# Two layers of a hybrid attention trunk: the second score product of each head over all 128 rows

## The chip, the cores and the metric

The kernel runs on one core of one Trainium2 chip. The metric is device time in microseconds (us) of one execution; the kernel before takes 760.22 us, the median of three runs (759.8, 760.22 and 763.26).

## The reference

The program computes two decoder layers over 512 tokens of width 1024, in float32, and a last norm. With h the residual, each layer is:

```
u = rmsnorm(h) @ w_in             # splits into qa ka va ga qd kd vd gd, 512 columns each
oa = 8 heads of 64: causal softmax(qa ka^T / 8) with a dilated-window mask, times va
od = 4 heads: (softmax(q1 k1^T / 8) - lam * softmax(q2 k2^T / 8)) times vd, then a norm
h = h + concat(oa * silu(ga), od * silu(gd)) @ w_out
h = h + (p @ w_ple) * sigmoid(rmsnorm(h) @ w_gate)
```

The first 16 channels of each 64 of q and k get a rotary embedding. Seen as scores, a layer has 16 heads of 64 channels: 8 in the differential mixer (two for each of its 4 heads) and 8 in the dilated one.

## The kernel before, in words

All products carry float32 operands in two parts: a high part in a rounded 32-bit format and a low part, which is the remainder. A product of two such operands takes three passes, high by high, high by low, low by high (`PASSES`).

The tensor engine's work is cut into units. A unit of projection (`unit`, L237 to L251) is 24 matmuls with 512 columns each (L248). A layer has 48 units in 12 chunks of 512 output columns, in the order of `SEQ`: v, q and k of the differential mixer (units 0 to 11), v, q and k of the dilated mixer (12 to 23), the two gates, the output product, the embedding's gate. The weights of a chunk come in four pairs of row blocks: SyncE (SP) loads a pair, ScalarE (ACT) writes the high part into a ring of five slots (L200), GpSimd (POOL), and VectorE (DVE) in one case out of eight after the start, subtracts to get the low part (L203).

Attention is laid between the projection's matmuls. Each of the 16 heads of a layer has a place near its own unit: `QD` for the differential heads (7.6 to 14.6), `QA` for the dilated ones (19.6 to 26.6). A head's score work (`softmax_rows`) is four blocks of 128 queries; block i has 128 * (i + 1) keys. Blocks 0 and 1 stand together, blocks 2 and 3 stand alone, each after a few projection matmuls. The scores of a block are two matmuls into the same bank (L392, L393). DVE then masks them and takes the extreme of each row (L399), ACT takes exp and the row sums (L404), DVE scales (L445, or L478 and L479, where two heads are combined). About 1.5 units after a head's scores, the tensor engine transposes the probabilities (L427), ACT and DVE split them into two parts (L431, L434), and the products with v follow (L456 for dilated heads, L495 for differential ones).

Two heads share a pair of 64-row halves. When the projection of q or k for a pair is finished (`qk_done`), DVE shuffles and multiplies (L552, L553), POOL adds the rotary part (L556, L557), ACT writes the high part to a staging tile (L560), DVE the low part (L563), and SP copies parts to where the scores read them (`move`, L178). For a pair, `QK` holds five tiles of 128 rows by 512 tokens. Tiles 0 and 1 are q of the two heads: high part in the head's own 64 rows, low part in the other 64. Tiles 2 and 3 hold the high part of k twice, so that one matmul over 128 rows gives both high by high and low by high (L392). Tile 4 holds the low part of k of both heads, written there by DVE directly, head e in rows 64e to 64e + 63. The high part of q by the low part of k is the second matmul (L393), over the head's own 64 rows. `QK` has two such buffers, for alternate pairs.

The order of instructions on each engine is fixed by hand: every piece has a place and a length in us, and `Plan.run` sorts them by those. Nothing is reordered afterwards. SP's queue carries all transfers, weights and the copies of q and k alike.

At the start, `setup` clears two tiles on DVE and builds the identity for transposes on POOL, while the first loads are on their way; eleven matmuls warm the tensor engine's clock up.

Of the kernel before, what the change touches and what calls it, by code (L numbers as in the profile page):

```python
# [9 lines left out]
F32 = mybir.dt.float32  # L10
F32R = mybir.dt.float32r
# [19 lines left out]


def const_tables():
    """Tables that depend on the shapes alone: rotary angles by channel and position, and the
    additive masks of the scores."""
    half = ROPE_DIM // 2
    inv = np.power(np.float32(ROPE_THETA),
                   -np.arange(half, dtype=np.float32) * np.float32(2.0 / ROPE_DIM)).astype(np.float32)
    ang = (np.arange(S, dtype=np.float32)[:, None] * inv[None, :]).astype(np.float32)
    cos, sin = np.cos(ang).T, np.sin(ang).T  # L40
    c = np.ones((128, S), np.float32)
    s = np.zeros((128, S), np.float32)
    for h in (0, 64):
        c[h:h + half] = cos
        c[h + half:h + ROPE_DIM] = cos
        s[h:h + half] = -sin
        s[h + half:h + ROPE_DIM] = sin
    r = np.arange(128)[:, None]
    k = np.arange(512)[None, :]
    dist = 384 + r - k  # L50
    mult = (((dist >= 0) & (dist <= 128)).astype(np.int64) + ((dist >= 0) & (dist % 4 == 0))
            + ((dist >= 0) & (dist % 16 == 0)))
    ma = np.where(mult > 0, 8.0 * np.log(np.maximum(mult, 1)), NEG).astype(np.float32)
    md = np.where(dist >= 0, 0.0, NEG).astype(np.float32)
    return np.ascontiguousarray(np.stack([c, s, ma, md], axis=1))


class Plan:
    """The order of the instructions. The tensor engine's pieces of work have a place t, counted in
    units of projection, and a length in us; the other engines' work has a place and a distance in us  # L60
    from the time at which the tensor engine gets there when nothing holds it."""

    def __init__(self):
        self.pieces, self.items = [], []
# [18 lines left out]
            f(*a)  # L83


# A layer's chunks of 512 columns, in their order; each is four units of projection.
SEQ = ["vd", "d0", "d1", "va", "a0", "a1", "gd", "ga", "o0", "o1", "p0", "p1"]
# Where the heads' scores, their transposed probabilities and the products with v come.
QD = [7.6, 8.6, 9.6, 10.6, 11.6, 12.6, 13.6, 14.6]
QA = [19.6, 20.6, 21.6, 22.6, 23.6, 24.6, 25.6, 26.6]  # L90
LT, LP, LO = 1.5, 2.15, 1.3
# Passes of a product of two operands in two parts.
PASSES = ((0, 0), (0, 1), (1, 0))
# Columns where the blocks of keys of a transposed head begin.
TO = [0, 512, 896, 1152]


def trunk(tc, x, p, attn_gain, w_in, w_out, lq1, lk1, lq2, lk2, subln, ple_gain, w_gate, w_ple,
          final_gain, tables, out):
    nc = tc.nc  # L100
# [4 lines left out]
    with tc.tile_pool(name="sb", bufs=1) as sb, tc.tile_pool(name="ps", bufs=1, space=PSUM) as psp, \  # L105
# [3 lines left out]
        RING = sb.tile([128, NPAIR, 2, 2, 512], F32R, name="ring")  # L109
        NSTG = 3  # L110
        STG = sb.tile([128, NSTG, 2, 512], F32, name="stg")
        QK = sb.tile([128, 2, 5, 512], F32R, name="qk")
        NT = sb.tile([128, 3, 512], F32R, name="nt")
        FR = sb.tile([128, 12 * 512], F32, name="fr")
        PT = sb.tile([128, 2, 1280], F32R, name="pt")
# [61 lines left out]
        def move(dst, src):  # L177
            nc.sync.dma_start(dst.bitcast(F32), src.bitcast(F32))  # L178

# [1 line left out]
        loads = []  # L181

        def add_pair(t, us, src, hi, lo, eng):
            loads.append((t, us, src, hi, lo, eng))

        def stage(n):
            # the fourth pair comes while the others are still on their way
            return OF[:, 4:6, :] if n == NSTG else STG[:, (n - (n > NSTG)) % NSTG]

        def emit_loads():  # L190
# [40 lines left out]
                return RING[:, slots[kb // 2], lo, kb % 2, :]  # L231
            return w

# [1 line left out]
        nunit = [0]  # L235

        def unit(s, w, ureg, kind, idx, done, k0=0, cols=slice(0, 512), length=1.0):  # L237
# [12 lines left out]
                pe(s + length * i / 8, 0.648 * length, part, i)  # L250
            done(s + 0.99 * length, o)  # L251

# [1 line left out]
        def sumsq(t, h, eng=ACT):  # L254
            acc = SS[:, 2 * t + h:2 * t + h + 1]
            if eng is ACT:
# [36 lines left out]
        def load_gain(i, src):  # L293
            nc.sync.dma_start(GN[i], src.partition_broadcast(128))

# [1 line left out]
        def setup():  # L297
            DVE.memset(PT[:, 0, 0:512].bitcast(F32), 0.0)
            DVE.memset(NHALF, -0.5)
            ACT.activation(ST[:, 132:136], NHALF, AF.Exp)  # L300
            make_identity(nc, IDT)

# [7 lines left out]
        def first_gain():  # L310
            POOL.partition_broadcast(GN[0], GROW)

        # the tensor engine's clock rises while the first loads are on their way
        def warm_up():
            b = bank()
            for i in range(NWARM):
# [24 lines left out]
                                         tmp[:, 2 * l:2 * l + 1], op0=OP.add, op1=OP.subtract)  # L341
                DVE.tensor_scalar(GSUB[l], GSUB[l], 0.5 * (1.0 - li), None, op0=OP.mult)

        # times from the start of the tensor engine's first work
        def st(us, f, *a):
            at(-10, 60 + us, f, *a)

# [18 lines left out]
                at(t - 1, 0.1 * h, sumsq, t, h, (ACT, DVE)[h])  # L366
            norm_T(t - 1, 1.0, t - 0.2, t, GN[0], 0)

# [1 line left out]
        nP = [0]  # L370
        nst = [0]

        def softmax_rows(b, pr, e, mask):
            """Scores of one head for all queries, masked, with their maximum; exp and its sums."""
            r = {}
            buf = QK[:, pr % 2]
            q, k1, k2 = buf[:, e], buf[:, 2 + e], buf[:, 4]
            a = slice(64 * e, 64 * e + 64)

            def qk(i):  # L380
                if i == 0:
                    r["P"] = PB[nP[0] % 3]
                    nP[0] += 1
                    s = HST[:, 16 * (nst[0] % 4):16 * (nst[0] % 4) + 16]
                    nst[0] += 1
                    r["m"], r["d"], r["r"] = (s[:, 4 * j:4 * j + 4] for j in range(3))
                if i in (0, 2, 3):
                    r["b"] = bank()
                o = r["b"][:, 128:384] if i == 1 else r["b"][:, 0:(i + 1) * 128]
                r[i] = o  # L390
                n = (i + 1) * 128
                mm(o, q[:, i * 128:(i + 1) * 128], k1[:, 0:n], start=True, stop=False)  # L392
                mm(o, q[a, i * 128:(i + 1) * 128], k2[a, 0:n], start=False, stop=True)  # L393

            def pq(i):
                return r["P"][:, QOFF[i]:QOFF[i] + (i + 1) * 128]

            def mx(i):
                DVE.tensor_tensor_reduce(pq(i), r[i], mask[:, 512 - (i + 1) * 128:], scale=-0.125,  # L399
                                         scalar=3.0e38, op0=OP.add, op1=OP.min,  # L400
                                         accum_out=r["m"][:, i:i + 1])

            def ex(i):
                ACT.activation(pq(i), pq(i), AF.Exp, bias=r["m"][:, i:i + 1], scale=-1.0,  # L404
                               accum_out=r["d"][:, i:i + 1])

            def rec():
                DVE.reciprocal(r["r"], r["d"])
            for i in range(4):
                pe(b + (0.0, 0.01, 0.13, 0.26)[i], (0.11, 0.22, 0.33, 0.43)[i], qk, i)  # L410
                at(b + (0.01, 0.01, 0.13, 0.26)[i], 0.1 + 0.05 * i, mx, i)
                at(b + 0.26, (0.3, 0.7, 1.2, 1.8)[i], ex, i)
            at(b + 0.26, 2.6, rec)
            r["pq"] = pq
            return r

        def transposed(tb, r):
            """P transposed, by block of keys, in two parts."""
            bk = {}
            W, O = [512, 384, 384], [0, 512, 896]  # L420

            def tr(g):
                bk[g] = bank()
                c = 0
                for j in ((0,), (1,), (2, 3))[g]:
                    for i in range(j, 4):
                        nc.tensor.transpose(bk[g][:, c:c + 128], r["pq"](i)[:, j * 128:(j + 1) * 128], IDT)  # L427
                        c += 128

            def hi(g):  # L430
                ACT.activation(PT[:, 0, O[g]:O[g] + W[g]], bk[g][:, :W[g]], AF.Copy)  # L431

            def lo(g):
                DVE.tensor_sub(PT[:, 1, O[g]:O[g] + W[g]], bk[g][:, :W[g]], PT[:, 0, O[g]:O[g] + W[g]])  # L434
            for g in range(3):
                pe(tb + 0.13 * g, (0.436, 0.327, 0.327)[g], tr, g)
                at(tb + 0.13 * g, 0.1, hi, g)
                at(tb + 0.13 * g, 0.65, lo, g)
# [98 lines left out]
            pe(e + LO, 0.436, tr)  # L537
            at(e + LO, 0.1, ev3)

# [1 line left out]
        SHUF = list(range(8, 16)) + list(range(8)) + list(range(16, 32))  # L541
        nrt = [0]

        def qk_done(pr, isk):
            def done(t, o):
                r = {}
# [13 lines left out]
                    ACT.activation(NT[:, 2 * isk], r[0][0], AF.Copy)  # L560

                def lo():
                    DVE.tensor_sub(buf[:, 4] if isk else NT[:, 1], r[0][0], NT[:, 2 * isk])  # L563

                # each head's stack of 128 rows: both parts of q, and the high part of k twice
                def place_hi():
                    for e in range(2):
                        src = NT[64 * e:64 * e + 64, 2 * isk]
# [73 lines left out]
                    at(s, 1.9, sumsq, t, h)  # L642
            return done

        # the last tile of tokens: its last columns in two steps, the norm's gain before its scale
        def last_norm(s):
            a, b = slice(0, 256), slice(256, 512)
            acc = [SS[:, 8 + i:9 + i] for i in range(2)]
# [30 lines left out]
            at(s + 0.99, 1.9, scale)  # L679
            at(s + 0.99, 2.0, finish)  # L680

# [1 line left out]
        for l in range(DEPTH):  # L683
            B = UNITS * l
            X, Y = l % 2, 1 - l % 2
# [84 lines left out]
                for e in range(2):  # L770
                    head_a(l, B, pr, e, Y)

            # h of the residual comes back
            def reload(t, l=l):
                nc.sync.dma_start(HT(t), (x2 if l == 0 else hsave)[t * 128:(t + 1) * 128, :])
            for t in range(T):
                at(B + 29.6 + 0.1 * t, 0, reload, t)

            # the layer's own embedding in two parts, halved for the gate's form, and its weights
            def load_p(l=l):  # L780
                nc.sync.dma_start(PTF, p[l])

# [21 lines left out]


def layout(name, a):
    """Weights as the chunks of 512 columns that the program loads, each partition's part of two
    blocks of rows in one run; p with its channels first."""
    a = np.asarray(a)
    if name == "p":  # L810
        a = a[:, 0].transpose(0, 2, 1).reshape(DEPTH, 2, 128, S).transpose(0, 2, 1, 3)
# [30 lines left out]
```

## Time and profile before

| what | value |
|---|---|
| median of the runs | 760.22 us |
| profiled execution: span from the first to the last instruction | 758.0 us |
| around that span, by the median of the runs | 2.2 us |
| tensor engine matmul busy | 732.0 us, 97% of the span |
| DVE, ACT, POOL busy | 59%, 45%, 46% |
| granted tensor clock, mean | 0.986 |
| L392 and L393, number of matmuls | 128 and 128 |

The profile gives no other time of the profiled execution than its span, so the 2.2 us around it are the median less the span. Busy times of the tensor engine (PE) overlap, because one matmul starts before the one ahead of it has left the array: what a matmul costs is read from the distance between its start and the next start. PEld is the loading of the stationary operand, which can run under the matmul ahead.

### The profile page before, as it was taken

How to read it: one execution, taken by the hardware profiler on the slowest of the kernel's cores; microseconds unless marked ns; L12 is line 12 of the kernel's file. 1: busy time of each engine (PE TensorE's matmuls, PEld its weight loads, DVE VectorE, ACT ScalarE, POOL GpSimd, SP SyncE). 2: the span in 40 equal slices, each digit the busy share in tenths (PEclk: the TensorE clock that was granted, in tenths of full speed). 3: DMA queues.
4: the chain of work that ended last, by engine and by line, in shares of the span. 5: the costliest groups of instructions: out<-in, count | busy, mean ns of one | idle time of the engine just before them, and what ended most of it. 6: DMA issues, size and time to landing. Idle time of an engine off the chain costs nothing.

```text
span 758.0 us, 9739 instructions
## 1 busy us (share of the span) xinstructions
PE 732.0 (97%) x3379; PEld 574.2 (76%) x3379; DVE 445.4 (59%) x935; ACT 342.1 (45%) x739; POOL 352.3 (46%) x275
## 2 busy tenths in 40 slices
PE   2899999999999999999999999999999999999996
PEld 1677777787777787888888767778777778788885
DVE  0874877557785653462473387756677665346344
ACT  2343364735565632453343246563456473335321
POOL 1357464268460514572364755516837042467132
PEclk7799999999999999999999999999999999999998
DMA  5425524036350154440341453403534114543102
GB/s 222 145 83 134 148 76 126 29 111 181 71 147 20 57 195 166 140 138 29 138 155 69 140 153 83 125 29 112 166 71 147 35 57 172 189 139 116 51 29 83
DMA packets 30882, 84.78 MB, mean 112 GB/s; under 512 B 5617, under 2 KB 5617, under 8 KB 30834
## 3 DMA queue, kind: packets, MB, share of 16 engines
q1 hardware_dynamic: 30834, 84.17, 35.9%
q8 instruction: 26, 0.43, 0.2%
q14 instruction: 22, 0.18, 0.1%
HBM read 63.18 MB, written 4.19 MB: 89 GB/s over the span
## 4 chain that ended last, share of the span: by engine, by line
PE 88%; issue 4%; DVE 3%; POOL 2%; ACT 1%; DMA 1%; SPq 0%; POOLq 0%; DVEq 0%
PE b L248 66%; PE b L393 6%; PE b L392 3%; PE b L427 3%; PE b L456 3%; PE b L495 3%; PE b L726 3%; POOL ring L203 2%; PE b L280 2%; DVE fr L268 1%; DMA stg<-in_w_in_dram 1%; ACT ring L200 1%; POOL st L265 0%; DVE of L607 0%; DVE ring L203 0%
## 5 line engine op out<-in xcount | busy, mean ns | idle before, releaser
L203 POOL TENSOR_TENSOR ring<-stg,ring 128x512 fp32r<-128x512 f32 x164 | 234.8, 1461 | 200.7 <-ACT ring L200 188.1
L248 PE MATMUL b<-xy,ring 128*128 128x512 f32 x1152 | 307.2, 404 | 0.6 <-POOL ring L203 0.6
L248 PE MATMUL b<-ring,xy 128*128 128x512 f32 (+1 forms) x1176 | 286.5, 393 | 0.6 <-POOL ring L203 0.5
L248 PEld LDWEIGHTS b<-ring,xy 128*128 128x128 f32 x1176 | 213.6, 189 | 47.6 <-POOL ring L203 2.8
L248 PEld LDWEIGHTS b<-xy,ring 128*128 128x128 f32 x1152 | 203.5, 188 | 50.0 <-issue 11.1
L200 ACT ACTIVATE ring<-stg 128x1024 fp32r<-128x1024 f32 x95 | 99.0, 1054 | 29.4 <-PE b L248 21.0
L404 ACT ACTIVATE fr<-fr,st 128x128 f32<-128x128 f32 (+3 forms) x128 | 70.8, 555 | 43.4 <-DVE st L399 43.1
L399 DVE CUSTOM_DVE_ANT_0 fr<-b,ct 128x128 f32<-128x128 f32 (+3 forms) x128 | 58.7, 485 | 47.0 <-PE b L393 46.8
L556 POOL TENSOR_TENSOR fr<-fr,ct 128x512 f32<-128x512 f32 x32 | 41.3, 1291 | 75.9 <-DVE fr L552 75.9
L268 DVE SCALAR_TENSOR_TENSOR fr<-fr,st,of 128x512 f32<-128x512 f32 x38 | 39.2, 1067 | 26.4 <-POOL st L265 26.4
L257 ACT ACTIVATE fr<-fr 128x512 f32<-128x512 f32 x35 | 22.1, 632 | 68.2 <-DVE fr L623 32.9
L393 PE MATMUL b<-qk 64*128 64x128 f32 (+3 forms) x128 | 52.4, 409 | 0.0
L434 DVE TENSOR_TENSOR pt<-b,pt 128x384 fp32r<-128x384 f32 (+1 forms) x72 | 41.0, 592 | 13.9 <-ACT pt L431 13.6
L393 PEld LDWEIGHTS b<-qk 64*128 64x128 f32 x128 | 23.4, 183 | 29.7 <-issue 24.8
L560 ACT ACTIVATE nt<-fr 128x512 fp32r<-128x512 f32 x32 | 20.1, 628 | 56.4 <-POOL fr L557 56.1
L392 PE MATMUL b<-qk 128*128 128x128 f32 (+3 forms) x128 | 42.9, 335 | 0.0
L557 POOL TENSOR_TENSOR fr<-fr 128x512 f32<-128x512 f32 x32 | 41.2, 1288 | 2.5
L265 POOL TENSOR_TENSOR st<-st 128x1 f32<-128x1 f32 x19 | 10.9, 576 | 65.3 <-DVE st L263 50.6
L431 ACT ACTIVATE pt<-b 128x384 fp32r<-128x384 f32 (+1 forms) x72 | 35.8, 522 | 7.5 <-PE b L427 6.9
L635 DVE SCALAR_TENSOR_TENSOR of<-of,b 128x512 f32<-128x512 f32 (+1 forms) x17 | 11.1, 655 | 46.3 <-ACT of L634 46.3
L427 PE MATMUL b<-idt,fr 128*128 128x128 f32 x240 | 37.9, 272 | 0.0
L427 PEld LDWEIGHTS b<-idt,fr 128*128 128x128 f32 x240 | 30.5, 140 | 8.8
(85 smaller groups left out, 702.4 us busy)
## 6 DMA issues: line engine op xcount, KB each, us to landing
stg<-in_w_in_dram SPq DMA_DIRECT2D x63, 512.0 KB, 3.6
qk<-nt SPq DMA_DIRECT2D x128, 128.0 KB, 2.3
stg<-in_w_out_dram SPq DMA_DIRECT2D x16, 512.0 KB, 3.3
stg<-in_w_ple_gate_dram SPq DMA_DIRECT2D x16, 512.0 KB, 3.5
fr<-in_x_dram SPq DMA_DIRECT2D x7, 512.0 KB, 7.6
stg<-in_w_ple_dram SPq DMA_DIRECT2D x4, 512.0 KB, 3.3
hsave<-fr SPq DMA_DIRECT2D x4, 512.0 KB, 2.7
fr<-hsave SPq DMA_DIRECT2D x4, 512.0 KB, 7.8
```

The costliest lines, as they stand in the source:

```text
L200: ACT.activation(hi, st, AF.Copy)
L203: eng[k].tensor_sub(lo[:, k], st[:, k], hi[:, k])
L248: mm(o, a, b, start=(i == 0 and n == 0), stop=(i == KB - 1 and n == 2))
L268: DVE.scalar_tensor_tensor(XN(t, h), H(t, h), RS[:, t:t + 1], gain[:, 512 * h:512 * (h + 1)], op0=OP.mult, op1=OP.mult)
L392: mm(o, q[:, i * 128:(i + 1) * 128], k1[:, 0:n], start=True, stop=False)
L393: mm(o, q[a, i * 128:(i + 1) * 128], k2[a, 0:n], start=False, stop=True)
L399: DVE.tensor_tensor_reduce(pq(i), r[i], mask[:, 512 - (i + 1) * 128:], scale=-0.125, scalar=3.0e38, op0=OP.add, op1=OP.min, accum_out=r["m ...
L404: ACT.activation(pq(i), pq(i), AF.Exp, bias=r["m"][:, i:i + 1], scale=-1.0, accum_out=r["d"][:, i:i + 1])
L427: nc.tensor.transpose(bk[g][:, c:c + 128], r["pq"](i)[:, j * 128:(j + 1) * 128], IDT)
L434: DVE.tensor_sub(PT[:, 1, O[g]:O[g] + W[g]], bk[g][:, :W[g]], PT[:, 0, O[g]:O[g] + W[g]])
L556: POOL.tensor_mul(r[0][1], r[0][1], SN)
L557: POOL.tensor_add(r[0][0], r[0][0], r[0][1])
```

## The change

`QK` gets a sixth tile for each buffer. Tiles 4 and 5 now hold the low part of k of head 0 and head 1 of a pair, each in its own 64 rows, and the other 64 rows of each are zero. The second matmul of a block reads all 128 rows of q and of that tile; the rows with the low part of q meet zeros. DVE writes the low part of k with two subtractions of 64 rows by 512 in place of one of 128 rows by 512. The zeros are written once, by four POOL memsets of 64 by 512 in `setup`, ahead of the identity. The scratch space for DMA descriptors is set to 1 KB per partition.

```diff
-        QK = sb.tile([128, 2, 5, 512], F32R, name="qk")
+        QK = sb.tile([128, 2, 6, 512], F32R, name="qk")
...
             DVE.memset(NHALF, -0.5)
+            for i in range(2):
+                for e in range(2):
+                    POOL.memset(QK[64 - 64 * e:128 - 64 * e, i, 4 + e].bitcast(F32), 0.0)
...
-            q, k1, k2 = buf[:, e], buf[:, 2 + e], buf[:, 4]
-            a = slice(64 * e, 64 * e + 64)
+            q, k1, k2 = buf[:, e], buf[:, 2 + e], buf[:, 4 + e]
...
                 mm(o, q[:, i * 128:(i + 1) * 128], k1[:, 0:n], start=True, stop=False)
-                mm(o, q[a, i * 128:(i + 1) * 128], k2[a, 0:n], start=False, stop=True)
+                mm(o, q[:, i * 128:(i + 1) * 128], k2[:, 0:n], start=False, stop=True)
...
                 def lo():
-                    DVE.tensor_sub(buf[:, 4] if isk else NT[:, 1], r[0][0], NT[:, 2 * isk])
+                    if not isk:
+                        DVE.tensor_sub(NT[:, 1], r[0][0], NT[:, 0])
+                        return
+                    for e in range(2):
+                        a = slice(64 * e, 64 * e + 64)
+                        DVE.tensor_sub(buf[a, 4 + e], r[0][0][a], NT[a, 2])
...
-    nc = _bacc.Bacc("TRN2", target_bir_lowering=False, num_devices=1)
+    nc = _bacc.Bacc("TRN2", target_bir_lowering=False, num_devices=1, dynamic_dma_scratch_size=1024)
```

The rest of the diff takes comments away.

## The prediction

> **What bounds the kernel now.** I read the page's chain of waits first, then the groups by line and shape, then the order of time on the tensor engine around one head's scores.
>
> ```profile
> span 758.0 us, 9739 instructions
> PE 88%; issue 4%; DVE 3%; POOL 2%; ACT 1%; DMA 1%; SPq 0%; POOLq 0%; DVEq 0%
> PE b L248 66%; PE b L393 6%; PE b L392 3%; PE b L427 3%; PE b L456 3%; PE b L495 3%; PE b L726 3%; POOL ring L203 2%; PE b L280 2%; DVE fr L268 1%; DMA stg<-in_w_in_dram 1%; ACT ring L200 1%; POOL st L265 0%; DVE of L607 0%; DVE ring L203 0
> ```
>
> The end is set by PE for 88% of the span. The two score products have the same columns and the same count, yet L393 holds 6% of the chain and L392 only 3%. The groups by shape show where the two differ:
>
> ```profile
> L392 PEld LDWEIGHTS b<-qk 128*128 128x128 f32 x128 | 24.0, 187 | 5.6
> L393 PEld LDWEIGHTS b<-qk 64*128 64x128 f32 x128 | 23.4, 183 | 29.7 <-issue 24.8 <-DVE fr L479 0.4 <-DVE fr L478 0.4
> L393 PE MATMUL b<-qk 64*128 64x512 f32 x32 | 15.8, 494 | 0.0
> L392 PE MATMUL b<-qk 128*128 128x512 f32 x32 | 12.7, 396 | 0.0
> ```
>
> A load over 64 rows takes as long as one over 128 (183 and 187 ns), but the loader stands idle for 29.7 us ahead of the L393 loads, nearly all of it "issue": no other engine is waited for. The matmul behind it shows 494 ns against 396. In order of time, for the first head of layer 0:
>
> ```profile
> 71.46 0.22 PE L392 MATMUL b<-qk 128*128 128x128 f32 x1
> ...
> 72.49 0.96 PE L248 MATMUL b<-xy,ring 128*128 128x512 f32 x3
> 73.29 0.34 PE L392 MATMUL b<-qk 128*128 128x384 f32 x1
> 73.56 0.44 PE L393 MATMUL b<-qk 64*128 64x384 f32 x1
> 73.92 0.96 PE L248 MATMUL b<-xy,ring 128*128 128x512 f32 x3
> 74.72 0.40 PE L392 MATMUL b<-qk 128*128 128x512 f32 x1
> 75.05 0.49 PE L393 MATMUL b<-qk 64*128 64x512 f32 x1
> 75.47 1.89 PE L248 MATMUL b<-xy,ring 128*128 128x512 f32 x7
> ```
>
> From start to start, L392 with 512 columns takes 75.05 - 74.72 = 0.33 us and L393 takes 0.42. The same widths where every load has 128 rows:
>
> ```profile
> 46.42 25.21 PE b L248 x111
> 196.89 1.21 PE L456 MATMUL b<-pt,xy 128*128 128x512 f32 x6
> 197.94 0.40 PE L392 MATMUL b<-qk 128*128 128x512 f32 x1
> 199.49 0.33 PE L456 MATMUL b<-pt,xy 128*128 128x128 f32 x2
> 199.66 0.91 PE L248 MATMUL b<-xy,ring 128*128 128x512 f32 x3
> ```
>
> The first row is the chain's: 25.21 / 111 = 0.227 us for 512 columns. L456, the product with v, runs exactly the widths of one head's scores, in pairs into one bank: 512, 512, 384, 384, 256, 256 in 197.94 - 196.89 = 1.05 us, and 128, 128 in 0.17. So every passage from 128 rows to 64 and back costs time before the array streams again, and the L248 behind the passage pays too.
>
> **The change part by part.** *The full-row product.* One head's scores now take (72.49 - 71.46) + (73.92 - 73.29) + (75.47 - 74.72) = 1.03 + 0.63 + 0.75 = 2.41 us. At the L456 spacing they would take 1.05 + 0.17 = 1.22. The three L248 behind a passage take 73.29 - 72.49 = 0.80 in place of 3 x 0.227 = 0.68; a head has three such returns, 3 x 0.12 = 0.36, of which I take 0.33, since some of it also follows L456 (199.66 to 200.40 in the same view). Gain for a head: 2.41 - 1.22 + 0.33 = 1.52 us; 32 heads give 48.6 us. Both ends: a second product that still loads in the open would keep the 0.42 spacing and gain nothing; the upper end is 48.6, as nothing in a stream goes below the L456 spacing. I take the upper end for the gross gain, because L456 is the same work in the same form.
>
> *What the gain runs into.* All engines have a fixed order, so PE can only keep a gain if what it waits for moves up too. Two of a layer's stages are dense on DVE and POOL. First the differential heads:
>
> ```profile
> 71.00:113.00 42.00, 42.00 (x179) 29.91 (x178) 32.58 (x83) 22.50 (x59) 24.60 (x19) 1.00 0.43 118
> 71.83 7.18 POOL L203 TENSOR_TENSOR ring<-stg,ring 128x512 fp32r<-128x512 f32 x5
> 78.97 1.29 POOL L556 TENSOR_TENSOR fr<-fr,ct 128x512 f32<-128x512 f32 x1
> 80.34 1.28 POOL L557 TENSOR_TENSOR fr<-fr 128x512 f32<-128x512 f32 x1
> 82.31 2.40 SPq L178 DMA_DIRECT2D qk<-nt  x4
> qk<-nt SPq DMA_DIRECT2D x128, 128.0 KB, 2.3
> 87.97 0.22 PE L392 MATMUL b<-qk 128*128 128x128 f32 x1
> ```
>
> Columns of the first row: PE, PEld, DVE, ACT and POOL busy, granted clock, DMA. PE is busy all 42 us, DVE 32.58 of them, at a clock of 1.00. POOL works without a break from 71.83 to 81.62, and that run starts before the first head has gained anything, so the k of the second pair is not rotated earlier. Its last copy is issued at about 82.31 + 3 x 0.6 = 84.1 and lands 2.3 later, at 86.4. The next head's scores start at 87.97, so 1.6 us of slack are left, and by then two heads have gained 3.0: PE waits about 1.4. DVE hangs on the same run:
>
> ```profile
> 82.31 0.69 DVE L563 TENSOR_TENSOR qk<-fr,nt 128x512 fp32r<-128x512 f32 x1 [0.83 <-ACT nt L560]
> 90.89 0.75 DVE L479 SCALAR_TENSOR_TENSOR fr<-fr,st 128x512 f32<-128x512 f32 x1
> 93.47 0.60 PE L427 MATMUL b<-idt,fr 128*128 128x128 f32 x4
> ```
>
> L563, the low part of k, waits there for ACT, which waits for POOL. The reductions of head 1 are queued behind it, then exp on ACT, then the combination that ends at 91.64; the transposes at 93.47 have 1.8 us of slack. Three heads' gain is 4.5, so PE waits 2.7 in all (the 1.4 included), and up to 0.7 more by the split described below: I take 3.1, between 2.0 (POOL's run gets shorter) and 4.5 (nothing moves). What is late next is the fourth pair's k:
>
> ```profile
> 110.41 7.66 POOL L203 TENSOR_TENSOR ring<-stg,ring 128x512 fp32r<-128x512 f32 x5
> 121.36 2.38 SPq L178 DMA_DIRECT2D qk<-nt  x4
> 128.41 0.22 PE L392 MATMUL b<-qk 128*128 128x128 f32 x1
> ```
>
> The copies land at 121.36 + 1.8 + 2.3 = 125.5, with 2.9 us of slack against another 4.5 gained by heads 3 to 5: 1.6 more, between 0 and 3. In the dilated stage the same run comes once:
>
> ```profile
> 187.10 2.39 SPq L178 DMA_DIRECT2D qk<-nt  x4
> 193.62 0.22 PE L392 MATMUL b<-qk 128*128 128x128 f32 x1
> ```
>
> Landing 191.2, slack 2.4 against 3.0: 0.6, and I allow 0.4 for the products with v that wait for L434 there; between 0 and 3. A layer gives back 3.1 + 1.6 + 1.0 = 5.7, both 11.4; by the ends above between 2 x 2.0 = 4 and 2 x 10.5 = 21.
>
> *The low part of k in two halves.* A second DVE instruction for each of 16 k.
>
> ```profile
> L563 DVE TENSOR_TENSOR qk<-fr,nt x16: 681/693/1671, 67.0 to 588.7; 128x512 fp32r<-128x512 f32 x16
> L463 DVE TENSOR_TENSOR of<-b,misc 64x512 f32<-64x512 f32 x16 | 10.9, 681 | 0.2
> ```
>
> A subtraction on 64 rows costs what one on 128 costs (L463, 681 ns), so DVE gets 16 x 0.69 = 11.0 us more, up to 16 x 1.67 = 26.7 if each takes the longest time seen. Queued behind it are the next head's reductions (L399), for which ACT's exp waits. Most of it lies in DVE's idle time (42.00 - 32.58 = 9.4 us in the stage above); what does not is in the 3.1. Uncovered, it would cost the 11.0. The Trainium skill, "SBUF — State Buffer", section "SBUF: two separate sides", says that a DVE operation with two SBUF inputs and a GpSimd operation that reads SBUF lock each other out for a whole instruction. The spread from 681 to 1671 in the row above agrees with such a lock without proving it; by it each new half could meet one POOL operation of 1.29, and an estimate from that row is 16 x 1.29 = 20.6 us more on DVE, and a time of up to 723 + 21 = 744.
>
> *The memsets and the scratch.*
>
> ```profile
> 0.72 0.21 POOL masks.py:197 MEMSET idt<- 128x128 f32 x1 [0.29 <-POOLq L830]
> 8.73 1.30 POOL L311 PARTITION_BROADCAST of<-misc  x1 [7.21 <-DMA stg<-in_w_in_dram]
> ```
>
> Four memsets of four times that width cost 4 x 0.21 at least and 4 x 1.3 = 5.2 at most, the time of a tensor operation of that width (L557). POOL idles 7.21 us before L311, so I take nothing; uncovered, they cost what exceeds that idle time. Queued behind them is the identity, whose first reader is a transpose after 20 us. The scratch size changes no instruction; all copies shown are SP's. I take nothing. A gain is excluded, as the copies are hidden now; a loss of 1 us in each landing would come out at the three dense places of each layer, 6 us, and that is the other bound.
>
> *Sum.* 758.0 - 48.6 + 11.4 = 720.8 us of span, plus the 2.2 by which the median of the runs exceeds the span: **723 us**.
>
> **The rivals.** *All of it is kept* (711.6 = 760.2 - 48.6): if the POOL runs shrink with the gain. For it: in the windows from 113 on DVE and POOL have room. Against: POOL's run from 71.83 starts before any gain.
>
> *DVE sets the pace.* The order on DVE with the added halves makes PE wait in every pair, not only in the dense stages: 21 us given back plus the 11.0 of the halves, less 4 that the 21 holds already (0.7 at three places in two layers), makes 28: 758.0 - 48.6 + 28 + 2.2 = 740. For it: 32.58 of 42 us busy. Against: in that row DVE still has 9.4 us idle against 5 x 1.52 = 7.6 gained and about 2 added.
>
> *Rows do not matter.* If the time of a matmul goes by columns alone and the open load belongs to the second product itself, the spacing stays 0.42 and the time 760. Against it: L456 accumulates pairs in one bank as well, at 0.17 to 0.23, and the L248 after L393, which has 128 rows, is late too. The Trainium skill, "TensorE: Matmul & The Clock Gate", section "Why this matters for your kernels", states this rule: a matmul over 32 rows takes the time of one over 128. The load rows (183 and 187 ns) agree with it, the spacing of 0.42 against 0.227 does not.
>
> *Slower.* One mechanism: the second half of L563 delays L399 and so each pair's exp and transposes by one full subtraction, in the open. Price 16 x 0.69 = 11.0, so 771. It decides only where the product's gain stays below 11.0 / 32 = 0.34 us a head, that is, if the passage cost is not removed. Against it: the 1.52 above.
>
> *The change doesn't do what it says*, that is, the loads stay in the open with 128 rows: priced like the third, 760.
>
> **How the numbers follow.** The forecast, 723 within 716 to 733 (4 to 21 us given back), 0.52; all kept, 0.22; DVE sets the pace, 0.18; no change, the third and the fifth together, 0.05; slower, 0.03. The range reaches from 711 (all kept) to 742 (DVE's pace and a little above it). What a measurement of this kernel can tell from no change is about 0.5%, 3.8 us: faster 0.92, same 0.05, slower 0.03, from the same cases.
>
> **What would show it.** L393 with 128 rows, its loads' idle time by "issue" near L392's 5.6 us, and 0.227 from start to start at 512 columns: the gross gain is right. A head's first L392 to the first L248 behind blocks 0 and 1 takes about 0.45 in place of 1.03. PE or its loader then shows waits that were not there: L392 for the copies of k and L427 for L479, some 3 us a layer near heads 2 and 6. L563 counts 32 for k with 64 rows, near 0.69 each. The forecast is wrong if the 0.42 spacing stays (time 760), if no such waits come (712), or if waits for DVE come at every pair (740).

## The result and the profile after

The changed kernel takes 740.92 us (median; 740.35 to 742.79) against 760.01 us on the same chip: ratio 0.975, 95% interval 0.9726 to 0.9773. It is faster by 19 us, where the forecast was 37 and a time of 723.

Page of the changed kernel: span and chain of waits.

```profile
span 738.4 us, 9759 instructions
PE 54%; DVE 15%; POOL 10%; issue 10%; ACT 5%; DMA 3%; SPq 1%; POOLq 0%; DVEq 0%; ACTq 0%
```

PE held 88% of the chain before and holds 54% now; DVE and POOL together hold a quarter. Groups by shape, changed kernel (L394 and L395 are the old L392 and L393):

```profile
L394 PEld LDWEIGHTS b<-qk 128*128 128x128 f32 x128 | 24.2, 189 | 6.2 <-issue 1.5 <-DMA qk<-nt 1.5
L395 PEld LDWEIGHTS b<-qk 128*128 128x128 f32 x128 | 24.2, 189 | 3.2
L395 PE MATMUL b<-qk 128*128 128x512 f32 x32 | 12.6, 393 | 0.0
```

The idle time ahead of the second product's loads fell from 29.7 to 3.2 us, and its matmul shows 393 ns, as the first one does. The first head of layer 0 in order of time:

```profile
74.68 0.22 PE L394 MATMUL b<-qk 128*128 128x128 f32 x1
...
75.14 0.85 PE L248 MATMUL b<-xy,ring 128*128 128x512 f32 x3
75.83 0.33 PE L394 MATMUL b<-qk 128*128 128x384 f32 x1
76.00 0.34 PE L395 MATMUL b<-qk 128*128 128x384 f32 x1
76.18 0.86 PE L248 MATMUL b<-xy,ring 128*128 128x512 f32 x3
76.87 0.39 PE L394 MATMUL b<-qk 128*128 128x512 f32 x1
77.10 0.39 PE L395 MATMUL b<-qk 128*128 128x512 f32 x1
77.33 1.98 PE L248 MATMUL b<-xy,ring 128*128 128x512 f32 x8
```

Both products stand 0.23 us apart at 512 columns. The scores of the head take 0.46 + 0.35 + 0.46 = 1.27 us (2.41 before), and the three L248 behind them 75.83 - 75.14 = 0.69 (0.80 before, at three places in a head, so 3 x 0.11 = 0.33). That is 1.14 + 0.33 = 1.47 us a head, 47.0 us for 32. The product does what it was expected to do; 28 of the 47 us are given back elsewhere.

Where, by the start of the first L248 of a unit in the two traces:

| from, to | before | changed | gain | 1.47 x heads |
|---|---|---|---|---|
| start of the span to the first projection | 23.32 | 26.54 | -3.2 | 0 |
| layer 1, unit 7 to 16 (8 differential heads) | 82.82 | 78.10 | 4.7 | 11.8 |
| layer 1, unit 19 to 27 (8 dilated heads) | 80.32 | 73.42 | 6.9 | 11.8 |

Layer 0 shows the same two gains, 4.5 and 6.9; outside these stages the distance between the kernels changes by 0.1 us at most. So there are three losses against 1.47 us a head: 3.2 us at the start, 7 us in each differential stage, 5 us in each dilated one. The start and two of the new waits, changed kernel in order of time:

```profile
0.72 2.20 POOL L302 MEMSET qk<- 64x512 f32 x4 [0.29 <-POOLq L838]
13.59 1.30 POOL L314 PARTITION_BROADCAST of<-misc  x1 [9.93 <-issue]
21.66 0.59 POOL L265 TENSOR_TENSOR st<-st 128x1 f32<-128x1 f32 x1 [6.77 <-issue]
89.95 0.30 PE L394 MATMUL b<-qk 128*128 128x128 f32 x1 [1.12 <-DMA qk<-nt]
96.49 0.33 PE L429 MATMUL b<-idt,fr 128*128 128x128 f32 x1 [0.85 <-DVE fr L481]
```

The broadcast starts 4.9 us later than before (8.73). The waits at 89.95 and 96.49 are the two that the prediction named for this place, the second pair's k and the combination of the first head. They are not the whole: over both layers, this is what the tensor engine waits for between matmuls (us in all, times, the longest; L429 are transposes of probabilities, L458 products with v of the dilated heads, L481 the combination and L436 the split of the probabilities on DVE):

```profile
PE b L429 <- DVE fr L481: 5.3, 8, 0.9
PE b L458 <- DVE pt L436: 5.3, 6, 1.3
PE b L248 <- POOL ring L203: 2.8, 8, 0.7
PE b L394 <- DMA qk<-nt: 2.2, 2, 1.1
```

Before, of these four only the wait for weights (L203) was there, with 1.1 us. Half of the waiting for DVE stands in the dilated stage, ahead of the products with v.

### The profile page after: what moved, and what is told of

Read it like the earlier page. It is cut to its first block, busy times and chain, and to the rows that moved or that the text cites. A ratio compares the mean times of both kernels' runs of the same rounds, so it can differ in the third digit from the quotient of the medians.

```text
span 738.4 us, 9759 instructions
## 1 busy us (share of the span) xinstructions
PE 692.6 (94%) x3379; PEld 571.1 (77%) x3379; DVE 464.9 (63%) x951; ACT 339.4 (46%) x739; POOL 355.3 (48%) x279
## 3 DMA queue, kind: packets, MB, share of 16 engines
q1 hardware_dynamic: 30834, 84.17, 37.2%
## 4 chain that ended last, share of the span: by engine, by line
PE 54%; DVE 15%; POOL 10%; issue 10%; ACT 5%; DMA 3%; SPq 1%; POOLq 0%; DVEq 0%; ACTq 0%
PE b L248 43%; POOL ring L203 7%; DMA stg<-in_w_in_dram 3%; PE b L734 3%; ACT fr L406 2%; PE b L429 2%; DVE qk L570 2%; PE b L280 2%; POOL fr L559 2%; PE b L458 2%; DVE fr L481 2%; DVE fr L401 2%; DVE pt L436 1%; DVE fr L447 1%; DVE fr L268 1%
## 5 line engine op out<-in xcount | busy, mean ns | idle before, releaser
L203 POOL TENSOR_TENSOR ring<-stg,ring 128x512 fp32r<-128x512 f32 x164 | 235.3, 1464 | 184.6 <-ACT ring L200 175.5
L248 PE MATMUL b<-xy,ring 128*128 128x512 f32 x1152 | 301.3, 399 | 1.8 <-POOL ring L203 1.4
L248 PE MATMUL b<-ring,xy 128*128 128x512 f32 (+1 forms) x1176 | 284.8, 392 | 1.6 <-POOL ring L203 1.5
L248 PEld LDWEIGHTS b<-ring,xy 128*128 128x128 f32 x1176 | 214.2, 189 | 46.4 <-POOL ring L203 4.8
L248 PEld LDWEIGHTS b<-xy,ring 128*128 128x128 f32 x1152 | 208.2, 189 | 40.6 <-POOL ring L203 5.4
L401 DVE CUSTOM_DVE_ANT_0 fr<-b,ct 128x128 f32<-128x128 f32 (+3 forms) x128 | 56.7, 484 | 10.1 <-PE b L395 9.7
L570 DVE TENSOR_TENSOR qk<-fr,nt 64x512 fp32r<-64x512 f32 x32 | 31.9, 996 | 28.5 <-ACT nt L562 28.1
L429 PE MATMUL b<-idt,fr 128*128 128x128 f32 x240 | 41.0, 278 | 5.9 <-DVE fr L481 5.3
L436 DVE TENSOR_TENSOR pt<-b,pt 128x384 fp32r<-128x384 f32 (+1 forms) x72 | 40.8, 590 | 8.4 <-ACT pt L433 7.6
L429 PEld LDWEIGHTS b<-idt,fr 128*128 128x128 f32 x240 | 31.1, 141 | 17.5 <-DVE fr L481 7.7
L265 POOL TENSOR_TENSOR st<-st 128x1 f32<-128x1 f32 x19 | 10.9, 573 | 64.1 <-DVE st L263 51.0
L394 PE MATMUL b<-qk 128*128 128x128 f32 (+3 forms) x128 | 39.6, 322 | 2.2 <-DMA qk<-nt 2.2
L395 PE MATMUL b<-qk 128*128 128x128 f32 (+3 forms) x128 | 41.1, 321 | 0.0
L280 PE MATMUL b<-idt,fr 128*128 128x128 f32 x128 | 20.4, 283 | 20.3 <-DVE fr L268 20.2
```

The costliest lines, as they stand in the source:

```text
L203: eng[k].tensor_sub(lo[:, k], st[:, k], hi[:, k])
L248: mm(o, a, b, start=(i == 0 and n == 0), stop=(i == KB - 1 and n == 2))
L395: mm(o, q[:, i * 128:(i + 1) * 128], k2[:, 0:n], start=False, stop=True)
L570: DVE.tensor_sub(buf[a, 4 + e], r[0][0][a], NT[a, 2])
```

## The experiments

My theory after the result: DVE, with the split low part of k, holds back the quick product, and the memsets delay the start. The rival: POOL's runs of weights and rotation hold it back, and the split is covered, as predicted. Eight runs take the change apart.

**The memsets on DVE.**

```diff
-                    POOL.memset(QK[64 - 64 * e:128 - 64 * e, i, 4 + e].bitcast(F32), 0.0)
+                    DVE.memset(QK[64 - 64 * e:128 - 64 * e, i, 4 + e].bitcast(F32), 0.0)
```

> The changed kernel with its four memsets on DVE in place of POOL, nothing else. Theory: the changed kernel's first projection starts 3.2 us later because the memsets stand on POOL ahead of the partition broadcast and of what delays it; on DVE they lie in idle time. The time falls by 3.2 us, to 737.5 (737 to 738.5), and the first L248 starts at 23.3 us again. Rival: the late start comes from the larger tile or the smaller scratch; the time stays at 741 and the first L248 at 26.5.

Measured 737.51 us, ratio 0.9698 (0.9684 to 0.9712) to before, and the first L248 starts 3.4 us earlier than in the changed kernel. POOL at the start, memsets on DVE:

```profile
9.12 1.30 POOL L314 PARTITION_BROADCAST of<-misc  x1 [7.60 <-DMA stg<-in_w_in_dram]
18.22 0.59 POOL L265 TENSOR_TENSOR st<-st 128x1 f32<-128x1 f32 x1 [7.80 <-issue]
```

The power (L265, the inverse root in the first norm, which the first projection needs) comes at 18.22 in place of 21.66. The memsets on POOL cost 740.9 - 737.5 = 3.4 us.

**The memsets on POOL, behind the broadcast.**

```diff
             DVE.memset(NHALF, -0.5)
-            for i in range(2):
-                for e in range(2):
-                    POOL.memset(QK[64 - 64 * e:128 - 64 * e, i, 4 + e].bitcast(F32), 0.0)
...
         def first_gain():
             POOL.partition_broadcast(GN[0], GROW)
+            for i in range(2):
+                for e in range(2):
+                    POOL.memset(QK[64 - 64 * e:128 - 64 * e, i, 4 + e].bitcast(F32), 0.0)
```

> The changed kernel with its four memsets still on POOL, but behind the partition broadcast, where POOL shows 8.3 us of idle time by issue ahead of the first power. Theory: POOL's idle time at the start is no room, since what follows (the broadcast, the power) begins a fixed time after what stands ahead; the time stays 740 to 741, as in the changed kernel. Rival: the idle time there is room for 2.2 us of memsets: 737.5, as with the memsets on DVE.

Measured 738.06 us, ratio 0.971 (0.9694 to 0.9726) to before. The theory of this run falls: there is room. Whether for all of the memsets can't be told, as the interval overlaps the one with the memsets on DVE.

```profile
8.72 1.30 POOL L311 PARTITION_BROADCAST of<-misc  x1 [7.21 <-issue]
10.09 2.21 POOL L314 MEMSET qk<- 64x512 f32 x4
19.31 0.59 POOL L265 TENSOR_TENSOR st<-st 128x1 f32<-128x1 f32 x1 [7.02 <-issue]
```

The power now starts at 19.31, 0.9 behind its place in the kernel before (18.44), where memsets ahead of the broadcast put it at 21.66, 3.2 behind. In the eight traces without memsets on POOL it starts between 17.79 and 19.18, so the 3.2 are clear of that spread and the 0.9 hardly are. What the idle time is shows in the sequencer's records of these two lines: the kernel before, then the changed one, then this one.

```profile
L311 POOLq MODIFY_POOL_CONFIG  x2: 13/13/13, 1.5 to 1.5; - x2
L265 POOLq MODIFY_POOL_CONFIG  x2: 129/129/129, 10.0 to 10.0; - x2
18.44 0.59 POOL L265 TENSOR_TENSOR st<-st 128x1 f32<-128x1 f32 x1 [8.41 <-issue]
```

```profile
L314 POOLq MODIFY_POOL_CONFIG  x2: 4/4/4, 3.6 to 3.7; - x2
L265 POOLq MODIFY_POOL_CONFIG  x2: 129/129/129, 14.8 to 14.8; - x2
```

```profile
L265 POOLq MODIFY_POOL_CONFIG  x2: 4/4/4, 12.3 to 12.4; - x2
```

Ahead of the broadcast and again ahead of the power stands a MODIFY_POOL_CONFIG, and POOL's idle time begins with it: 1.5 to 8.73 and 10.0 to 18.44 in the kernel before, 3.7 to 13.59 and 14.8 to 21.66 in the changed one, 12.4 to 19.31 here. The Trainium skill, "GPSIMD Engine Reference", section "2.1 Instruction dispatch", says that the first call of freshly loaded code pays about 6 us after this instruction with nothing to see in the profile. The traces agree in kind: these three show 6.9 to 9.9 us, all ten traces 6.0 (1.5 to 7.55, the scratch alone) to 9.9. In both kernels with memsets on POOL this time began only when the memsets were through (3.7 and 12.4). Its length is not fixed, and here it was 1.5 us shorter than before, which hides most of the memsets in this trace. The broadcast also reads a load whose landing no trace shows, so its wait can be in part one for that load. Why the length varies, and whether it was shorter here because the memsets ran, was not found out.

**The halves alone.**

```diff
-                    DVE.tensor_sub(buf[:, 4] if isk else NT[:, 1], r[0][0], NT[:, 2 * isk])
+                    if not isk:
+                        DVE.tensor_sub(NT[:, 1], r[0][0], NT[:, 0])
+                        return
+                    for e in range(2):
+                        a = slice(64 * e, 64 * e + 64)
+                        DVE.tensor_sub(buf[a, 4], r[0][0][a], NT[a, 2])
```

> The kernel before with the low part of k written by two DVE subtractions of 64 rows, into the same tile; product, memsets and scratch as before. Theory: with the old product PE sets the pace and DVE has room, so the halves are covered: 760 to 763. Rival: the halves lie on the path everywhere, 16 x 0.69 to 16 x 1.0: 771 to 776.

Measured 759.81 us, ratio 1.0001 (0.9992 to 1.0011): nothing, though DVE is busy with the low part of k for 32.0 us in place of 15.2. Groups by shape, the kernel before, then this run:

```profile
L563 DVE TENSOR_TENSOR qk<-fr,nt 128x512 fp32r<-128x512 f32 x16 | 15.2, 948 | 21.4 <-ACT nt L560 21.4
```

```profile
L568 DVE TENSOR_TENSOR qk<-fr,nt 64x512 fp32r<-64x512 f32 x32 | 32.0, 1000 | 25.2 <-ACT nt L560 24.7
```

**The product alone.**

```diff
-                mm(o, q[a, i * 128:(i + 1) * 128], k2[a, 0:n], start=False, stop=True)
+                mm(o, q[:, i * 128:(i + 1) * 128], k2[:, 0:n], start=False, stop=True)
```

> The kernel before with the second score product over all 128 rows of the one tile with the low part of k, no zeros, no halves, no memsets: the scores get the low part of q by the other head's low part of k on top, so the output changes a little; the work is the full-row product alone. Theory: the halves of the changed kernel (31.9 us busy against 15.2) lie on DVE's path about 2 to 3 times in each stage, 4 to 5 us a layer, and the memsets cost 3.2: the time is 741 - 3.2 - 9 = 729 (725 to 732). Rival: POOL's runs and the fixed order set the pace without the halves: 737 to 738, as without the memsets alone.

Measured 721.24 us, ratio 0.9487 (0.9472 to 0.9501), below the expected 725 to 732. Of the 47.0 us, 39.0 are kept when the product comes without the halves and the memsets. Against 737.51 (halves, memsets out of the way) the halves cost 16.3 us here, and nothing under the old product. What the tensor engine waits for in the product alone (its line numbers are those of the kernel before; L427, L456, L392, L479 and L434 are L429, L458, L394, L481 and L436 of the changed kernel):

```profile
PE b L427 <- DVE fr L479: 2.8, 4, 0.9
PE b L248 <- POOL ring L203: 1.6, 6, 0.3
PE b L456 <- DVE pt L434: 0.6, 2, 0.3
PE b L392 <- DMA qk<-nt: 0.2, 1, 0.2
```

Without the halves the two waits for DVE are 3.4 us in place of 10.6. In the changed kernel's trace they stand at the first and third head of each stage, not at every pair.

**The zeros beside q.** The low part of k stays whole, and the high part of q is copied a third time, into a tile whose other rows are zero.

```diff
-        QK = sb.tile([128, 2, 5, 512], F32R, name="qk")
+        QK = sb.tile([128, 2, 7, 512], F32R, name="qk")
...
-            q, k1, k2 = buf[:, e], buf[:, 2 + e], buf[:, 4]
+            q, k1, k2, qz = buf[:, e], buf[:, 2 + e], buf[:, 4], buf[:, 5 + e]
...
-                mm(o, q[a, i * 128:(i + 1) * 128], k2[a, 0:n], start=False, stop=True)
+                mm(o, qz[:, i * 128:(i + 1) * 128], k2[:, 0:n], start=False, stop=True)
...
                         if isk:
                             move(buf[64 - 64 * e:128 - 64 * e, 2 + e], src)
+                        else:
+                            move(buf[64 * e:64 * e + 64, 5 + e], src)
...
```

> The same result as the changed kernel in another way: the low part of k stays in one tile, written by one DVE subtraction; the zeros stand beside a third copy of the high part of q (two more tiles for each buffer, two more copies by SP for each pair), which is the stationary operand of the second product. Memsets on DVE. Theory: DVE is relieved of the halves, and SP has room for 32 more copies of 0.6 us: 729 (725 to 733), the same as the product alone. Rival: the added copies come ahead of those of the low part of q and of k and make the scores wait 1.3 us in the dense places: 733 to 740.

Measured 721.46 us, ratio 0.949 (0.9476 to 0.9505): the same as the product alone, with the reference's result. The 32 more copies on SP cost nothing that can be told. This version beats both kernels.

**A second low part of k that nothing reads**, added to the kernel with the zeros beside q.

```diff
+        DUM = sb.tile([128, 512], F32R, name="dum")
...
                     DVE.tensor_sub(buf[:, 4] if isk else NT[:, 1], r[0][0], NT[:, 2 * isk])
+                    if isk:
+                        DVE.tensor_sub(DUM, r[0][0], NT[:, 2])
```

> The kernel with the zeros beside q (721.5 us), with the subtraction for the low part of k done a second time on DVE, into a tile that nothing reads: one DVE instruction of 128 by 512 more for each of 16 k, and nothing waits for its result. Theory: DVE's time sets the pace once the product is quick, whatever the instruction is for: 15 to 17 us more, as the halves cost, 736 to 739. Rival: the halves cost because the second head's part comes later, or because of their form; then the spare instruction costs little: 721 to 727.

Measured 734.64 us, ratio 0.9663 (0.9648 to 0.9678): 13.2 us more, for a result that nobody waits for. So it is DVE's time that is paid, not the place of the second head's part. It is less than the 15 to 17 expected. Where POOL leaves DVE alone, an instruction and its spare copy take 1.2 us together (83.94 to 85.15 below, in this run), and two halves about 1.4 in the changed kernel; at 16 times 0.2 that is about the 737.5 - 734.6 = 2.9 us by which the halves cost more, though no run shows it alone.

```profile
83.94 0.69 DVE L567 TENSOR_TENSOR qk<-fr,nt 128x512 fp32r<-128x512 f32 x1 [3.87 <-ACT nt L564]
84.55 0.69 DVE L569 TENSOR_TENSOR dum<-fr,nt 128x512 fp32r<-128x512 f32 x1
85.15 0.55 DVE L403 CUSTOM_DVE_ANT_0 fr<-b,ct 128x384 f32<-128x384 f32 x1
```

Why a half of 0.69 costs a full us on the mean: the memsets on DVE, dilated stage, DVE and POOL in order of time, then DVE at the same place with the low part whole (zeros beside q).

```profile
199.48 3.31 DVE L570 TENSOR_TENSOR qk<-fr,nt 64x512 fp32r<-64x512 f32 x2
199.25 2.99 POOL L203 TENSOR_TENSOR ring<-stg,ring 128x512 fp32r<-128x512 f32 x2 [1.70 <-ACT ring L200]
```

```profile
193.16 1.61 DVE L566 TENSOR_TENSOR qk<-fr,nt 128x512 fp32r<-128x512 f32 x1
```

The two halves run beside two POOL subtractions and last 3.31 us together; the whole one, beside the same two, lasts 1.61. In the differential stage, with no POOL operation beside them, two halves last 1.4 (the changed kernel, below).

```profile
437.73 1.41 DVE L570 TENSOR_TENSOR qk<-fr,nt 64x512 fp32r<-64x512 f32 x2 [3.87 <-ACT nt L562]
```

Beside POOL, each half stretches to about the length of one POOL operation. The Trainium skill, "SBUF — State Buffer", section "SBUF: two separate sides", gives the rule that would make it so (a DVE operation with two SBUF inputs and a GpSimd operation that reads SBUF keep each other out for a whole instruction); the traces agree, 3.31 beside 2.99, without having tested it alone.

How full DVE is can be misread. In the window from 175 to 216 us, first in the kernel before, then with the memsets on DVE, then in the product alone (columns as in the prediction):

```profile
175.00:216.00 41.00, 41.00 (x185) 29.79 (x183) 31.51 (x78) 22.68 (x54) 23.56 (x19) 1.00 0.42 117
```

```profile
175.00:216.00 41.00, 37.67 (x195) 30.54 (x194) 40.03 (x91) 23.41 (x61) 26.49 (x20) 1.00 0.45 120
```

```profile
175.00:216.00 41.00, 40.66 (x219) 34.26 (x218) 39.24 (x96) 24.59 (x61) 24.66 (x18) 1.00 0.52 145
```

With the halves DVE is busy for 40.03 of 41 us, where it was for 31.51, and PE no longer is all the time. But in the product alone DVE is nearly as full, 39.24, while PE is busy for 40.66: the faster kernels have other work in the same window, and a full DVE alone doesn't say that PE waits. Over the same work (units 19 to 27 of layer 0) DVE is busy for 58.2 of 80.3 us before, 60.1 of 69.4 in the product alone and 65.9 of 73.4 with the halves and the memsets on DVE. POOL's busy time there is 37.3 us in the product alone and 37.2 with the halves, so it is not POOL's work that the halves lengthen.

**The rotation without its sine product**, in the kernel with the zeros beside q.

```diff
                 def rot2():
-                    POOL.tensor_mul(r[0][1], r[0][1], SN)
                     POOL.tensor_add(r[0][0], r[0][0], r[0][1])
```

> The kernel with the zeros beside q (721.5 us) without the product with the sine table in the rotary embedding: 32 POOL operations of 1.29 us are left out, so the rotation is not the reference's. Theory: what the quick product still gives back (9.6 of 48.6 us) hangs on POOL's runs of weights and rotation ahead of the dense places; with runs 1.3 to 2.6 us shorter the time falls to 714 to 718. Rival: DVE's order alone sets it; 720 to 722.

Measured 714.92 us, ratio 0.9404 (0.9387 to 0.9421): 6.5 us less, so most of the last 8.0 us hangs on POOL's operations. Whether by the length of POOL's runs, by q and k being ready 1.3 us earlier, or by what POOL takes from DVE this run doesn't tell apart.

**The scratch alone.**

```diff
-    nc = _bacc.Bacc("TRN2", target_bir_lowering=False, num_devices=1)
+    nc = _bacc.Bacc("TRN2", target_bir_lowering=False, num_devices=1, dynamic_dma_scratch_size=1024)
```

> The kernel before with the DMA descriptor scratch of 1 KB, nothing else. Theory: no instruction changes and no queue of this kernel uses it: 760, within 0.3%. Rival: transfers land later at some of the dense places, up to 6 us more: 763 to 766.

Measured 759.86 us, ratio 0.9997 (0.9987 to 1.0008): nothing, as expected.

## Why the prediction was right and wrong

| term of the sum | forecast | measured | from |
|---|---|---|---|
| full-row product, gross | -48.6 | -47.0 | 1.47 us a head in the changed kernel |
| given back to POOL's runs and the fixed order | +10.6 | +8.0 | 47.0 - 39.0, the product alone |
| low part of k in halves | +0.8 (3.1 - 2.7 of a layer) | +16.3 | 737.5 - 721.2 |
| memsets | 0 | +3.4 | 740.9 - 737.5 |
| scratch | 0 | -0.2 | 759.9 against 760.1, within its interval |

With 760.0 before, the measured terms give 740.5; the kernel takes 740.9.

- *The gross gain was right*, in its cause too. The passage between 128 and 64 rows cost the time: with 128 rows the second product keeps the spacing of L456, and the L248 behind it comes on time. The rival by which rows do not matter is refuted here: the same columns went from 0.42 to 0.23 us. The Trainium skill, "TensorE: Matmul & The Clock Gate", section "Why this matters for your kernels", states the rule for a single matmul over 32 rows; it does not carry over to these products of 64 rows among those of 128. What a stream of 64-row products alone would take, no run shows.
- *What the order gives back came out near in total, 8.0 for 10.6, not in its parts.* The product alone keeps 8.5 us of a differential stage and 10.9 of a dilated one, by the starts of the units; the prediction's waits, without the share of the halves, left about 8 and 11. But of the waits that it named, in the product alone, the copies of the second pair's k cost 0.2 us (forecast 1.4) and the combination 0.9 (1.3). For the copies of the fourth pair (1.6) and of the dilated stage (0.6) PE shows no wait; it waits 0.55 for the third head's combination instead, and 0.3 for L434 (0.4). So the closeness of the total is partly luck.
- *The step that failed is the cover of the halves*: "most of it lies in DVE's idle time (42.00 - 32.58 = 9.4 us)". That idle time was read at PE's old pace. The gain takes the same time out of the window that the halves were to hide in. The prediction put the two beside each other among the rivals (7.6 gained and about 2 added, which is already more than the 9.4) and still charged the halves 0.4 us a layer, with 0.7 as the most. In the dilated stage it allowed 0.4 for L434 and did not read DVE's room; there PE waits 5.3 us for that line over both layers (L436), against 0.6 without the halves. And it took 0.69 us for a half although the row it quoted went up to 1.67. The 16 more instructions, at 32.0 - 15.2 = 16.8 us of DVE time, came out almost whole, as 16.3.
- *The memsets failed too*, by less: "POOL idles 7.21 us before L311, so I take nothing". That idle time follows a change of POOL's configuration; it moved with what stood ahead of it, and grew to 9.93.
- The main case, 716 to 733, did not come. The time lies where the rival "DVE sets the pace" put it (740, chance 0.18). Its core is what the runs show: the halves on DVE cost almost their whole time. Its figure is partly luck: it held 21 us for the order (8.0 measured), 7 more for the halves (16.3) and nothing for the memsets (3.4), which makes 28 against 27.7. And the sign that it gave, waits for DVE at every pair, came at two places of a stage.

## What to carry to other kernels

Idle time that is to hide added work must be read at the pace that the change brings, not at the one it takes away: when the bound engine gets quicker by 1.5 us a head, the next engine loses as much room. When padding with zeros makes a product uniform, ask which operand carries the zeros: here they were free beside the one that transfers put in place, and cost 16 us beside the one that a busy engine writes. A window of fixed times holds other work once the kernel is faster: compare the busy time of the same work, and the waits. Idle time called "issue" is not room until a run has put work there.

## What was not expected of the hardware

- One round from 128 rows to 64 and back costs about 0.40 us of PE at 384 or 512 columns: (0.33 - 0.23) + (0.42 - 0.23) + (0.80 - 0.69), about a quarter of it in the matmuls that follow.
- 2.2 us of POOL memsets ahead of the partition broadcast delay the first projection by 3.2 us; behind the broadcast they cost 0.55 us of the time (738.06 against 737.51), within the noise. The wait after each of these two changes of POOL's configuration took 6.0 to 9.9 us.
- A DVE subtraction costs the same for 64 rows as for 128, and stretches the same beside POOL (least, median, longest in ns), in the changed kernel and with the spare low part. So two halves cost twice one whole, both at the least and at the longest.

```profile
L570 DVE TENSOR_TENSOR qk<-fr,nt x32: 670/690/1690, 70.2 to 575.3; 64x512 fp32r<-64x512 f32 x32
```

```profile
L569 DVE TENSOR_TENSOR dum<-fr,nt x16: 678/684/1776, 68.3 to 569.5; 128x512 fp32r<-128x512 f32 x16
```
